# A two-block decoder on one core: mixer scores from plain fp32 data as head pairs, and the gated feed-forward's hidden part computed the other way round

## The chip, the cores and the metric

One core of a Trainium2 chip runs one program. The metric is the time of an execution on the device in microseconds (us). The kernel before was timed three times: median 1898.77 us (1898.02 to 1899.66). A separate execution was profiled.

## The reference, cut to what matters

256 tokens of width 1024 pass through 12 stages. Two layers of the first block, each: gated feed-forward, hybrid mixer, cross attention to a memory, gated feed-forward. Two layers of the second block, each: second mixer, feed-forward with squared ReLU. Before each stage stands an RMS norm, behind it another one and the residual sum. All data is fp32. The parts that the change touches:

```python
def swiglu(x, w_gate, w_up, w_down):            # w_gate, w_up: 1024 x 2816
    return (jax.nn.silu(x @ w_gate) * (x @ w_up)) @ w_down
# hybrid mixer: 8 query heads of 64, 2 key/value heads; keys and values also compressed
def compress(kv, pe, w1, w2):                   # 15 blocks of 32 tokens, per head
    ...
    return jax.nn.silu(flat @ w1) @ w2          # flat: 2048 wide, w1: 2048 x 256
s_c = einsum('bqgrd,bngd->bgrqn', qi, kc) * scale    # against 15 compressed keys
s_s = einsum('bqgrd,bqgmd->bgrqm', qi, ks) * scale   # against chosen blocks (here all)
s_w = einsum('bqgrd,bkgd->bgrqk', qi, kw) * scale    # against a window (here all)
# second mixer: 8 index heads and 8 attention heads of 64
logits = einsum('bqhd,bsd->bqhs', iq, ik) * 64 ** -0.5
s = einsum('bqhd,bqkhd->bqhk', q, k) * 64 ** -0.5
```

## The kernel before, in words

**Numbers.** TensorE has two ways of multiplying here. Weights and activations are split into two fp32r parts, high and low (`split`, L517; ScalarE writes the high part, VectorE the low one), and three products (high x low, low x high, high x high; `mm3`, L543) stand for one fp32 product. Plain fp32 operands are multiplied without a split; the profile shows each such product as two matmul records with a weight load each. A transpose is one record.

**Order.** The functions only record operations. `Recorder` (L145) then plans each engine's order with costs of its own (`cost`, L176) and buffers by tag (L499): 4 raw weight tiles, 6 each of `wH` and `wL`, and of the 8 PSUM banks 4 `acc`, 2 `mm`, 2 `tr`. Of the operations that are ready, TensorE takes the one recorded first. All loads go through SyncE's queue in program order. Every instruction is emitted at one line, L449, so groups are told apart by tiles.

**Weights.** `wunit` (L524) loads 256 rows of a weight matrix (512 KB) and splits them. `proj_gen` (L817) is a projection to up to 512 columns for both halves of 128 tokens: 4 units, and per half 24 matmuls with 512 columns, the activations `xT` as stationary operand. It yields after each unit, 8 times in all.

**Gated feed-forward** (`ffn`, L762; `ffn_like`, L708; four of the twelve stages). The 2816 hidden columns go in 11 chunks of 256. Chunk 0 uses `up` (L772): per token half 24 matmuls of 512 columns (gate and up side by side), SiLU and product on ScalarE and VectorE, and `hidden_T` (L755), two PE transposes and a split. Chunks 1 to 10 use `gemm_T` (L697): the weights are stationary and all 256 tokens move, so the hidden part comes out transposed, in 96 matmuls of 256 columns; `up_T` (L780) does the gating, for which `rstd_rows` (L688) makes a row copy of the norm factor, with two PE transposes per feed-forward. Then `down` of the chunk before takes 24 matmuls of 512 columns.

**Hybrid mixer** (`mix`, L993, two stages). Projections first, with `compress` (L1047) of keys and of values between them: 4 loads of 512 KB each, split; per load 8 matmuls of 256 columns whose stationary operand holds the high and the low part of the gathered blocks in 64 columns. Queries go to `stack` (L893): per parity of the heads one tile with the high part in one half of the 128 rows and the low part in the other. Keys (`dup_copy`, L1010) stand twice, high and low, in both halves of the rows. So a head's scores are two fp32r matmuls over 128 rows. Then per half of the tokens (L1203): compressed scores of 8 heads (8 records over `kcT`), softmax, and the head loop (L1240): scores against window and selected keys side by side (2 x 128 or 2 x 256 columns), softmax on VectorE and ScalarE, transposes, product with the values. `Fill` (L840) puts steps of other projections between the heads. Of the 4 `acc` banks, two hold the output sums, so two are left for scores.

**Second mixer** (`mix2`, L1327, two stages). Index scores (L1360): per head two fp32r matmuls, as above, with stacked queries. Attention (L1435): plain fp32 products over the 64 rows of a head; a group is two heads of the same parity, thus of the same half of the rows, in one bank. There are 4 groups per half of the tokens, with 128 keys for the first and 256 for the second.

## Time and profile before

| what | value |
|---|---|
| median of 3 runs | 1898.77 us |
| profiled execution, time | 1897.3 us |
| profiled execution, span | 1895.5 us |
| TensorE busy | 1873.8 us (99%) |
| TensorE clock granted | 0.999 of full speed |
| VectorE, ScalarE busy | 1260.9 us (67%), 1054.9 us (56%) |
| DMA | 332.13 MB, 54.4% of 16 engines' span |

The span is what the trace covers, from the first to the last instruction; the execution took 1.8 us more. A matmul's record is longer than the step to the next one, since matmuls are pipelined: what a matmul costs the stream is read from start to start.

### The profile page before, as it was taken

The page shows a single profiled execution, that of the slowest core. Times are in us where ns is not written, and L with a number is a line of the kernel's source. Part 1 is how long each engine was busy: PE and PEld are TensorE (multiplying, and loading weights), DVE is VectorE, ACT ScalarE, POOL GpSimd, SP SyncE. Part 2 cuts the span into 40 slices and gives each one's busy share as a digit, 9 for nine tenths or more (in the row PEclk, how much of TensorE's full clock was granted, in tenths as well). Part 3 has the DMA queues.
Part 4 walks back from the last instruction along what each step waited for, and adds up shares of the span by engine and source line. Part 5 has one row for each costly group of instructions (what it writes and reads, how often), then busy time and mean ns, then how long its engine had stood idle before and what let it go on. Part 6 is the DMA issues. An engine that isn't in the chain of part 4 may idle for free.

```text
span 1895.5 us, 30068 instructions
## 1 busy us (share of the span) xinstructions
PE 1873.8 (99%) x11452; PEld 1644.6 (87%) x11452; DVE 1260.9 (67%) x2194; ACT 1054.9 (56%) x1747; POOL 55.1 (3%) x82
## 2 busy tenths in 40 slices
PE   9999999999999999999999999999999999999998
PEld 7999788888999899988788889998789998788997
DVE  6655887766656665668967576557965556966554
ACT  5444775556444544457755664447665446565443
POOL 0000000200000000000011000000000000000000
PEclk9999999999999999999999999999999999999999
DMA  7555654454565566557444455565536555535653
GB/s 247 188 182 183 204 184 151 150 173 130 193 200 182 163 200 196 183 164 242 144 165 156 134 180 182 183 190 160 165 125 193 189 194 171 172 112 187 200 180 112
DMA packets 229569, 332.13 MB, mean 175 GB/s; under 512 B 17680, under 2 KB 123696, under 8 KB 229424
## 3 DMA queue, kind: packets, MB, share of 16 engines
q1 hardware_dynamic: 229424, 330.20, 54.4%
q8 instruction: 90, 1.47, 0.3%
q14 instruction: 55, 0.45, 0.1%
HBM read 329.10 MB, written 1.05 MB: 174 GB/s over the span
## 4 chain that ended last, share of the span: by engine, by line
PE 87%; DVE 7%; ACT 2%; DMA 2%; issue 1%; POOL 0%; SPq 0%; DVEq 0%; POOLq 0%; ACTq 0%
PE mm L449 36%; PE acc L449 31%; PE tr L449 20%; DVE wL L449 3%; DVE m L449 2%; ACT wH L449 1%; DVE s L449 1%; DVE sm L449 1%; DVE xT L449 1%; DMA raw<-in_w_in_dram 0%; DVE sc L449 0%; ACT xT L449 0%; DMA raw<-in_xa_wk_dram 0%; ACT junk L449 0%; DVE x L449 0%
## 5 line engine op out<-in xcount | busy, mean ns | idle before, releaser
L449 DVE TENSOR_TENSOR wL<-raw,wH 128x1024 fp32r<-128x1024 f32 (+3 forms) x612 | 732.1, 1200 | 235.0 <-ACT wH L449 231.6
L449 ACT ACTIVATE wH<-raw 128x1024 fp32r<-128x1024 f32 (+3 forms) x612 | 635.0, 1040 | 226.4 <-PE mm L449 92.6
L449 PE MATMUL acc<-wH,m 128*128 128x512 f32 (+1 forms) x1664 | 533.8, 392 | 0.6 <-DVE m L449 0.5
L449 PE MATMUL mm<-wH,xT 128*128 128x512 f32 (+2 forms) x1152 | 363.0, 384 | 6.2 <-DVE xT L449 3.5
L449 PEld LDWEIGHTS acc<-wH,m 128*128 128x128 f32 (+1 forms) x1664 | 309.0, 186 | 67.4 <-DVE m L449 2.4
L449 PE MATMUL acc<-wL,m 128*128 128x512 f32 (+1 forms) x864 | 331.6, 387 | 0.0
L449 PE MATMUL mm<-xT,wH 128*128 128x256 f32 x1792 | 323.0, 282 | 0.0
L449 PE MATMUL tr<-xT,wH 128*128 128x256 f32 x1664 | 299.1, 282 | 0.0
L449 PEld LDWEIGHTS mm<-xT,wH 128*128 128x128 f32 x1792 | 279.5, 190 | 3.7
L449 PEld LDWEIGHTS tr<-xT,wH 128*128 128x128 f32 x1664 | 259.1, 190 | 2.8
L449 PEld LDWEIGHTS mm<-wH,xT 128*128 128x128 f32 x1152 | 210.4, 188 | 49.5 <-DVE xT L449 10.0
L449 PE MATMUL mm<-xT,wL 128*128 128x256 f32 x896 | 250.6, 283 | 0.0
L449 PE MATMUL tr<-xT,wL 128*128 128x256 f32 x832 | 233.2, 283 | 0.0
L449 PE MATMUL mm<-wL,xT 128*128 128x512 f32 (+2 forms) x576 | 219.5, 381 | 0.4 <-DVE wL L449 0.2
L449 ACT ACTIVATE nat<-nat 128x512 f32<-128x512 f32 x68 | 42.9, 631 | 277.2 <-DVE nat L449 277.2
L449 PEld LDWEIGHTS acc<-wL,m 128*128 128x128 f32 (+1 forms) x864 | 159.0, 184 | 31.2
L449 PEld LDWEIGHTS mm<-xT,wL 128*128 128x128 f32 x896 | 169.3, 190 | 1.0
L449 PEld LDWEIGHTS tr<-xT,wL 128*128 128x128 f32 x832 | 157.4, 190 | 0.5
L449 PEld LDWEIGHTS mm<-wL,xT 128*128 128x128 f32 x576 | 108.5, 188 | 18.6 <-DVE wL L449 2.2
L449 POOL TENSOR_TENSOR sm<-sm,neghalf 128x1 f32<-128x1 f32 (+1 forms) x60 | 41.0, 683 | 1832.9 <-ACT sm L449 1678.4
L449 PE MATMUL mm<-wH,m 128*128 128x512 f32 x256 | 88.7, 406 | 0.0
L449 DVE TENSOR_TENSOR m<-acc,m 128x512 f32<-128x512 f32 (+1 forms) x64 | 39.7, 620 | 66.1 <-ACT junk L449 63.3
(158 smaller groups left out, 1610.7 us busy)
## 6 DMA issues: line engine op xcount, KB each, us to landing
raw<-in_w_ff_dram SPq DMA_DIRECT2D x128, 512.0 KB, 4.4
raw<-in_ffn_w_gate_dram SPq DMA_DIRECT2D x176, 256.0 KB, 3.4
raw<-in_ffn_w_up_dram SPq DMA_DIRECT2D x176, 256.0 KB, 3.8
raw<-in_ffn_w_down_dram SPq DMA_DIRECT2D x88, 512.0 KB, 5.3
raw<-in_w_in_dram SPq DMA_DIRECT2D x80, 512.0 KB, 4.0
raw<-in_w_out_dram SPq DMA_DIRECT2D x32, 512.0 KB, 3.6
raw<-in_cmp_w_dram SPq DMA_DIRECT2D x16, 512.0 KB, 4.6
raw<-in_xa_wk_dram SPq DMA_DIRECT2D x16, 512.0 KB, 5.7
```

Source lines behind the costliest of these rows:

```text
L449: getattr(getattr(self.nc, op.eng), op.name)(*[r(v) for v in op.args], **{k: r(v) for k, v in op.kw.items()})
```

## The change

The gated feed-forward no longer has an `up_T`: all its chunks use `up`, with weights moving in 512 columns and PE transposes of the hidden part. In the mixers queries and keys stay plain fp32 in 64 rows per head; two heads, one in each half of the rows, write to two banks one after the other (`SS`), and the second mixer's attention takes the two parities together likewise. `compress` multiplies plain data: each of four blocks of 128 rows has a stationary operand of 32 columns and writes its own 32 PSUM partitions; the four quarters are summed on VectorE. `compress` has become a generator that advances once per two steps of the query projection (keys) and of the gates' projection (values). The planner's cost of such matmuls is changed too. The diff, without some unchanged lines and four columns of indentation:

```diff
@@ -180,9 +180,11 @@
+        part = 0.6 if list(args[1].shadow.ap)[0][1] == 64 else 0.33 if m == 32 and n == 256 else 1.0
         if args[1].base.dtype == F32R or args[1].shadow.dtype == F32R:
             return max(0.4425 * n + 5.0, m / 1.2 + 4.0)
-        return 2 * max(2 * n / 2.4 + 3.0, m / 1.2 + 4.0)
+        return part * 2 * max(2 * n / 2.4 + 3.0, m / 1.2 + 4.0)
@@ -727,14 +730,14 @@
         h = T(tag, [128, nk, 256], F32R), T(tag, [128, nk, 256], F32R)
-        if c:
+        if c and up_T:
             banks = [P("mm" if c % 2 else "tr") for _ in range(2)]
...
             up_T([o.rearrange("p (j n) -> p j n", j=2) for o in banks], h, R)
-        for t in range(2 if c == 0 else 0):
-            if begin:
+        for t in range(0 if c and up_T else 2):
+            if c == 0 and begin:
@@ -777,15 +780,7 @@
-    def up_T(o, h, R):
-        g, hn = T("nat", [128, 2, 256]), T("nat", [128, 2, 256])
-        DVE.tensor_tensor(g, o[0], R, op=ALU.mult)
-        ACT.activation(g, g, AF.Silu)
-        DVE.tensor_tensor(g, g, R, op=ALU.mult)
-        DVE.tensor_tensor(hn, o[1], g, op=ALU.mult)
-        split(h[0], h[1], hn)
-    ffn_like(nch, load_up, up, up_T, load_down, 2, gains, xT, xTn, begin)
+    ffn_like(nch, load_up, up, None, load_down, 2, gains, xT, xTn, begin)
@@ -889,14 +884,6 @@
-def stack(dst, tr, t):
-    v, sl = tr.rearrange("p (k n) -> p k n", k=4), slice(t * 128, t * 128 + 128)
-    for par in range(2):
-        r, q = slice(par * 64, par * 64 + 64), slice(64 - par * 64, 128 - par * 64)
-        evict(dst[par][r, :, sl], v[r])
-        DVE.tensor_tensor(dst[par][q, :, sl], v[r], dst[par][r, :, sl].bitcast(F32), op=ALU.subtract)
@@ -994,7 +981,7 @@
-    KH, KL = (T("m4", [128, 2, 2, 256], F32R) for _ in range(2))
+    KK = T("m4", [128, 2, 2, 256])
@@ -1011,9 +998,8 @@
             r, q = slice(g * 64, g * 64 + 64), slice(64 - g * 64, 128 - g * 64)
-            for to in (r, q):
-                evict(KH[to, g, br, sl], tr[r, :])
-                DVE.tensor_tensor(KL[to, g, br, sl], tr[r, :], KH[r, g, br, sl].bitcast(F32), op=ALU.subtract)
+            evict(KK[r, g, br, sl], tr[r, :])
+            DVE.tensor_copy(KK[q, g, br, sl], tr[r, :])
@@ -1040,32 +1026,35 @@
                                   peT[:, q * 8:q * 8 + 8].unsqueeze(2).to_broadcast([128, 8, 15]), op=ALU.add)
-        GG = T("m4", [128, 16, 64], F32R)
-        split(GG[:, :, 0:32], GG[:, :, 32:64], G.rearrange("p j g n -> p j (g n)"))
-        return GG
-    def compress(i, GG):
+        return G
+    def compress(i, G, made):
         hp = P("acc")
...
             SP.dma_start(raw, a["cmp_w1"][l, i, u * 512:(u + 1) * 512, :].rearrange("(j p) n -> p j n", p=128))
-            H, L = T("wH", [128, 4, 256], F32R), T("wL", [128, 4, 256], F32R)
-            rec.background = True
-            split(H, L, raw)
-            rec.background = False
             for j in range(4):
-                k = 4 * u + j
-                PE.matmul(hp[:64, :256], GG[:, k, :], H[:, j, :], start=k == 0, stop=False)
-                PE.matmul(hp[:64, :256], GG[:, k, :], L[:, j, :], start=False, stop=k == 15)
+                PE.matmul(hp[32 * j:32 * j + 32, :256], G[:, 4 * u + j].rearrange("p g n -> p (g n)"), raw[:, j, :],
+                          start=u == 0, stop=u == 3, skip_group_check=True)
+            yield
         hn = T("hidn", [32, 256], bufs=2)
-        evict(hn, hp[32:64, :256])
-        DVE.tensor_tensor(hn, hn, hp[:32, :256], op=ALU.add)
+        evict(hn, hp[0:32, :256])
+        for r in (32, 64, 96):
+            DVE.tensor_tensor(hn, hn, hp[r:r + 32, :256], op=ALU.add)
         ACT.activation(hn, hn, AF.Silu)
...
         SP.dma_start(w2[:, :, 1, :], w2v)
-        return hn, w2
+        made += [hn, w2]
+    def side_by_side(proj_, other):
+        for i, _ in enumerate(proj_):
+            if i % 2:
+                next(other, None)
+        run(other)
@@ -1081,11 +1070,10 @@
     proj(w, 2840, 512, xT, dst_g)
-    hk, w2k = compress(0, GK)
-    qT = [T("m4", [128, 4, 256], F32R) for _ in range(2)]
+    qT = T("m4", [128, 4, 256])
@@ -1095,19 +1083,17 @@
                           rs.unsqueeze(2).to_broadcast([128, 8, 64]), op=ALU.mult)
-        tr = P("tr")
-        for k in range(4):
-            PE.transpose(tr[:, k * 128:k * 128 + 128], qn[:, k * 128:k * 128 + 128], ident)
-        stack(qT, tr, t)
-    proj(w, 0, 512, xT, dst_q)
+        transpose_f32(qT[:, :, t * 128:t * 128 + 128], qn, 4, on_act=True)
+    ck, cv = [], []
+    side_by_side(proj_gen(w, 0, 512, xT, dst_q), compress(0, GK, ck))
+    hk, w2k = ck
     hid = hidden(hk)
-    hv, w2u = compress(1, GV)
     kp = P("tr")
...
                   start=hf == 0, stop=hf == 1)
-    kc = T("kcT", [128, 2, 2, 16], F32R, bufs=1)
-    split(kc[:, :, 0], kc[:, :, 1], kp[:, :32].rearrange("p (g n) -> p g n", g=2))
+    kc = T("kcT", [128, 2, 16], bufs=1)
+    DVE.tensor_copy(kc, kp[:, :32].rearrange("p (g n) -> p g n", g=2))
@@ -1122,7 +1108,8 @@
     mT = memkv[("m", l)] = mem_prepare(l)
-    proj(w, 1024, 280, xT, dst_b2)
+    side_by_side(proj_gen(w, 1024, 280, xT, dst_b2), compress(1, GV, cv))
+    hv, w2u = cv
@@ -1205,17 +1192,18 @@
-        sc = P("acc")
-        for h in range(8):
-            PE.matmul(sc[:, h * 32:h * 32 + 32], qT[h % 2][:, h // 2, sl],
-                      kc[:, h // 4].rearrange("p r n -> p (r n)"), start=True, stop=True)
-        sv = sc[:, :256].rearrange("p (h r n) -> p h r n", h=8, r=2)
+        sc = [P("acc") for _ in range(2)]
+        for k in range(4):
+            for e in range(2):
+                r = slice(e * 64, e * 64 + 64)
+                PE.matmul(sc[e][:, k * 16:k * 16 + 16], qT[r, k, sl], kc[r, k // 2], start=True, stop=True)
         pc = T("s1", [128, 8, 32])
...
         pv = pc[:, :, 0:15]
-        DVE.tensor_tensor(pv, sv[:, :, 0, 0:15],
-                          cb[:, t * 16:t * 16 + 15].unsqueeze(1).to_broadcast([128, 8, 15]), op=ALU.add)
-        DVE.tensor_tensor(pv, pv, sv[:, :, 1, 0:15], op=ALU.add)
+        for e in range(2):
+            sv = sc[e][:, :64].rearrange("p (k n) -> p k n", k=4)
+            DVE.tensor_tensor(pc.rearrange("p (k e) n -> p k e n", e=2)[:, :, e, 0:15], sv[:, :, 0:15],
+                              cb[:, t * 16:t * 16 + 15].unsqueeze(1).to_broadcast([128, 4, 15]), op=ALU.add)
@@ -1239,10 +1227,14 @@
             g = h // 4
-            S = P("acc")
-            for i, KK in enumerate((KH, KL)):
-                PE.matmul(S[:, :2 * K].rearrange("p (b k) -> p b k", b=2), qT[h % 2][:, h // 2, sl],
-                          KK[:, g, :, 0:K], start=i == 0, stop=i == 1)
+            if h % 2 == 0:
+                SS = [P("acc") for _ in range(2)]
+                for e in range(2):
+                    r = slice(e * 64, e * 64 + 64)
+                    PE.matmul(SS[e][:, :2 * K].rearrange("p (b k) -> p b k", b=2), qT[r, h // 2, sl],
+                              KK[r, g, :, 0:K], start=True, stop=True)
+            S = SS[h % 2]
@@ -1327,8 +1319,8 @@
     idx = [T("m4", [128, 584]) for _ in range(2)]
-    iqT = [T("m4", [128, 4, 256], F32R) for _ in range(2)]
-    ikH, ikL = (T("ik", [128, 256], F32R, bufs=2) for _ in range(2))
+    iqT = T("m4", [128, 4, 256])
+    ik = T("ik", [128, 256])
@@ -1337,16 +1329,12 @@
             do_rope(idx[t][:, :576].rearrange("p (h d) -> p h d", d=64), t, 9)
-            tr = P("tr")
-            for k in range(4):
-                PE.transpose(tr[:, k * 128:k * 128 + 128], idx[t][:, k * 128:k * 128 + 128], ident)
-            stack(iqT, tr, t)
+            transpose_f32(iqT[:, :, t * 128:t * 128 + 128], idx[t][:, :512], 4, on_act=True)
             tr = P("tr")
...
             sl = slice(t * 128, t * 128 + 128)
-            for r in (slice(0, 64), slice(64, 128)):
-                evict(ikH[r, sl], tr[0:64, :128])
-                DVE.tensor_tensor(ikL[r, sl], tr[0:64, :128], ikH[0:64, sl].bitcast(F32), op=ALU.subtract)
+            evict(ik[0:64, sl], tr[0:64, :128])
+            DVE.tensor_copy(ik[64:128, sl], tr[0:64, :128])
@@ -1358,12 +1346,14 @@
         for h0 in (0, 1, 4, 5):
-            S = P("acc")
-            for j in range(2):
-                h = h0 + 2 * j
-                for i, kk in enumerate((ikH, ikL)):
-                    PE.matmul(S[:, j * K:j * K + K], iqT[h % 2][:, h // 2, sl], kk[:, 0:K],
-                              start=i == 0, stop=i == 1)
+            if h0 % 2 == 0:
+                SS = [P("acc") for _ in range(2)]
+                for j in range(2):
+                    for e in range(2):
+                        r = slice(e * 64, e * 64 + 64)
+                        PE.matmul(SS[e][:, j * K:j * K + K], iqT[r, h0 // 2 + j, sl], ik[r, 0:K],
+                                  start=True, stop=True)
+            S = SS[h0 % 2]
@@ -1433,12 +1423,15 @@
         for h0 in (0, 1, 4, 5):
-            S = P("acc")
+            if h0 % 2 == 0:
+                SS = [P("acc") for _ in range(2)]
+                for j in range(2):
+                    for e in range(2):
+                        r, hp = slice(e * 64, e * 64 + 64), h0 // 2 + j
+                        PE.matmul(SS[e][:, j * K:j * K + K], qT[r, hp, sl], kT[r, hp, 0:K], start=True, stop=True)
+            S = SS[h0 % 2]
             s = T("sc", [128, 2, K])
-            for j in range(2):
-                h = h0 + 2 * j
-                r = slice((h % 2) * 64, (h % 2) * 64 + 64)
-                PE.matmul(S[:, j * K:j * K + K], qT[r, h // 2, sl], kT[r, h // 2, 0:K], start=True, stop=True)
```

## Rows read from the trace of the kernel before

**Rows 1.** The page, parts 1 and 4: TensorE's busy row; the ending chain by engine.

```profile
PE 1873.8 (99%) x11452; PEld 1644.6 (87%) x11452; DVE 1260.9 (67%) x2194; ACT 1054.9 (56%) x1747; POOL 55.1 (3%) x82
...
PE 87%; DVE 7%; ACT 2%; DMA 2%; issue 1%; POOL 0%; SPq 0%; DVEq 0%; POOLq 0%; ACTq 0%
```

**Rows 2.** Ending chain in order of time: start us, length us, what; one chunk, ffn1.

```profile
58.31 11.42 PE mm L449 x96
69.73 5.58 PE acc L449 x24
```

**Rows 3.** PE timeline, an untransposed chunk: start us, us, instruction, count.

```profile
663.05 0.39 PE L449 MATMUL tr<-ident,s 128*128 128x128 f32 x2
663.19 0.48 PE L449 MATMUL mm<-wL,xT 128*128 128x512 f32 x1
663.51 0.63 PE L449 MATMUL mm<-wH,xT 128*128 128x512 f32 x2
```

**Rows 4.** PE timeline, second mixer's attention, scores with 128 keys, 64 rows.

```profile
1353.87 0.39 PE L449 MATMUL mm<-wH,xT 128*128 128x512 f32 x1
1354.19 0.71 PE L449 MATMUL acc<-m,m 64*128 64x128 f32 x4
1354.83 0.50 PE L449 MATMUL mm<-wH,xT 128*128 128x512 f32 x1
1355.16 0.39 PE L449 MATMUL mm<-wL,xT 128*128 128x512 f32 x1
```

**Rows 5.** PE timeline, the same with 256 keys.

```profile
1370.45 1.13 PE L449 MATMUL acc<-m,m 64*128 64x256 f32 x4
1371.51 0.50 PE L449 MATMUL mm<-wH,xT 128*128 128x512 f32 x1
```

**Rows 6.** PE timeline, first mixer, plain fp32 products with all 128 rows.

```profile
315.12 1.00 PE L449 MATMUL acc<-m,pT 128*128 128x64 f32 x8
315.93 0.48 PE L449 MATMUL mm<-wH,xT 128*128 128x512 f32 x1
316.24 0.39 PE L449 MATMUL mm<-wL,xT 128*128 128x512 f32 x1
```

**Rows 7.** PE timeline, first mixer, compression of the keys (32 records in all).

```profile
227.96 0.28 PE L449 MATMUL acc<-wH,m 128*64 128x256 f32 x1
...
231.65 0.40 PE L449 MATMUL mm<-wH,xT 128*128 128x512 f32 x1
```

**Rows 8.** PE timeline, first mixer, scores of the second tokens against compressed keys.

```profile
282.91 0.96 PE L449 MATMUL acc<-kcT,m 128*128 128x32 f32 x8
283.72 0.48 PE L449 MATMUL mm<-wH,m 128*128 128x512 f32 x1
284.04 0.39 PE L449 MATMUL mm<-wL,m 128*128 128x512 f32 x1
```

**Rows 9.** PE timeline, first mixer, one head's scores, 2 x 128 keys.

```profile
280.41 0.40 PE L449 MATMUL acc<-m,m 128*128 128x256 f32 x2
280.65 0.39 PE L449 MATMUL mm<-wH,m 128*128 128x512 f32 x1
```

**Rows 10.** PE timeline, first mixer, one head's scores, 2 x 256 keys.

```profile
308.17 0.71 PE L449 MATMUL acc<-m,m 128*128 128x512 f32 x2
308.72 0.40 PE L449 MATMUL mm<-wH,xT 128*128 128x512 f32 x1
```

**Rows 11.** PE timeline, second mixer, index scores with 256 keys.

```profile
1321.90 2.13 PE L449 MATMUL acc<-ik,m 128*128 128x256 f32 x14
1323.87 0.62 PE L449 MATMUL mm<-wH,xT 128*128 128x512 f32 x2
```

**Rows 12.** Who waited for whom, PE, whole span: us in total, times, longest us.

```profile
PE tr L449 <- DVE nat L449: 2.9, 5, 0.9
...
PE tr L449 <- DVE m L449: 1.3, 3, 0.5
```

**Rows 13.** DVE groups by form: count, busy us, mean ns, idle before: the weight splits.

```profile
L449 DVE TENSOR_TENSOR wL<-raw,wH 128x1024 fp32r<-128x1024 f32 x580 | 709.3, 1226 | 233.7 <-ACT wH L449 230.5
```

## What the change was predicted to do

> **What bounds the kernel.** I read the page first. TensorE is busy for 99% of the span, and the chain that ended last runs on it for 87% [rows 1]; the rest of that chain is short pieces at the seams. Then the chain in order of time: in the gated feed-forward it alternates 96 matmuls in 11.42 us and 24 in 5.58 us with nothing between [rows 2]. So the stream of TensorE is the time, and an edit is priced by what it adds to that stream or takes from it, start to start. Then the timeline, for the forms that the change adds. Two things are to be seen. First, leaving full-row matmuls for matmuls over 64 rows costs something. The fp32r matmul ahead of such a group takes 0.32 us to the next start, and the one behind it 0.33 [rows 4], where 0.23 is usual (5.58 / 24 [rows 2]); the group's four records take 0.64 [rows 4], where four full-row ones would take 4 x 0.111 = 0.45: eight of these take 0.81, and the next matmul 0.31, 0.08 too long [rows 6]. So 0.19 outside and 0.19 inside, 0.38 us per group of half-row matmuls. Full-row fp32 pays none of it [rows 6]. Second, a record costs 0.112 us at 128 columns and (1.06 - 0.19) / 4 = 0.216 at 256 [rows 5], so an estimate is 0.43 at 512; a plain product is two records.
>
> **The change, part by part.** The sum is made on the profiled execution, 1897.3 us, which is 1.5 under the median of the runs, 1898.77.
>
> *Gated feed-forward.* Chunks 1 to 10 of four stages: 96 matmuls, 11.42 us, go [rows 2]. In their place come 48 of 512 columns, twice the 24 of 5.58 us: 11.16 [rows 2]. To these come two pairs of transposes; a pair takes 0.14 us and makes the next matmul 0.32 instead of 0.23 long, 0.23 in all [rows 3]. That is 11.16 + 0.46 - 11.42 = +0.20 per chunk, +8.0 for 40 chunks. The two transposes of the row copy go in each stage, 4 x 0.23 = -0.9. Sum +7.1. VectorE and ScalarE lose work here, which TensorE's unbroken alternation already hid: worth nothing. Their new chain (SiLU, product, transposes, split) lies beside the other half's 24 matmuls or the `down` of the chunk before; without that cover it would show once per chunk.
>
> *Compression, per mixer.* Before, 32 matmuls in 3.69 us [rows 7], twice: 7.4. After, 8 groups of four products, two records of 0.216 each. Does the array run the four column quarters at once? No row shows it. Bounds: all at once 0.43 per group, one after the other 1.73. For entering the narrow form: nothing (the narrowest rows, 64 columns, enter and leave freely [rows 7], though over the whole array) or 0.38 as for half rows. I take all at once, since the four share neither operand nor partitions, and the 0.38, since these are tiles as the half rows are: 8 x 0.81 = 6.5, so -0.9. Ends: -4.0 and +9.5. With a free change of form the sum would be 16 x 0.38 = 6.1 us lower over both mixers. The Trainium skill (TensorEngine Tiling (Array Packing), Tiling Modes, Key Properties) says that changing the tiling mode drains the engine, and it names no exception for columns; that speaks against this change and for the sum with 0.38. Half rows agree with it [rows 4]; no row here shows narrow tiles.
>
> *Scores on half rows, per mixer.* Two heads of a pair use different halves and different banks; bounds are half of the serial time and all of it, and I take half, the rows' switch of 0.38 on top, since nothing is shared that a row shows to be busy. Compressed scores: before 0.81 + 0.08 per half of the tokens [rows 8], 1.8; after 2 x (8 x 0.112 + 0.38) = 2.6: +0.8 (serial +2.6). Head scores: before 0.24 per head [rows 9] and 0.55 [rows 10] less the 0.08 that a matmul behind transposes takes [rows 3], eight heads each: 1.9 + 3.7 = 5.6. After, four pairs per half: 4 x (0.43 + 0.38) + 4 x (0.86 + 0.38) = 8.2, +2.6 (serial 13.4, +7.8). So a first mixer changes by -0.9 + 0.8 + 2.6 = +2.5, two of them by +5.0.
>
> *Second mixer.* Index scores: before 16 x 0.14 [rows 11] and 16 x 0.11 [rows 8], 4.0; after two groups of four products per half, 2 x (0.45 + 0.38) + 2 x (0.86 + 0.38) = 4.1: +0.1 (serial +2.8). Attention: before four groups per half, each one switch: 4 x (0.45 + 0.38) + 4 x (0.86 + 0.38) = 8.3; after half as many groups with twice the products: 4.1, so -4.2 (serial 6.8, -1.5). Two mixers: -8.2.
>
> *What else moves.* The splits of 16 loads (1.23 us each on VectorE [rows 13], as much on ScalarE), half of the key copies, the query stacks and the split of the gathered blocks go: all beside TensorE's stream. The most that it can free are TensorE's waits for VectorE ahead of transposes, 2.9 + 1.3 us in the whole run [rows 12]; I book 0, as the copies that end them remain. The loads of `compress` now stand on SyncE's queue between the projection's, and a raw tile comes free only when TensorE has read it; each has a full step of the projection ahead of it. For the values they also stand behind the loads of the memory, which ran ahead of the gates' projection alone. On ScalarE the values' SiLU now comes among the gates' exponentials, and three small adds follow each compression; the steps of the other projections cover that. POOL's queue is passed by nothing.
>
> Sum: 7.1 + 5.0 - 8.2 = +3.9 us, 1901.2 in the profiled execution, **1902.7** as a median. A measurement of this kernel tells about 0.2%, 3.8 us, from no change, so this lies on the edge.
>
> **Rivals.** *Only neighbours overlap.* The two records of a product sit in the same tile, so if records start and end in their order, only the last of one head and the first of the next run together: n products take n + 1 record times, not n. Then compression takes 8 x (5 x 0.216 + 0.38) = 11.7 (+4.3), compressed scores +1.0, head scores 4 x (0.65 + 0.38) + 4 x (1.30 + 0.38) = 10.8 (+5.2), index scores +0.8, attention -3.5: 7.1 + 2 x 10.5 - 2 x 2.7 = +22.7, 1921. For it: all records of a form in the trace do follow one another. Against it: none of them had another half to run in. The Trainium skill (TensorE: Matmul & The Clock Gate, Part 3) says that matmuls start and end strictly in order while tiles overlap; by that rule it is this case, and no row here can show it.
>
> *Banks come free apart.* With two banks for scores, the second of a pair is free only when VectorE has read the odd head. Where TensorE has nothing recorded earlier to do, it takes the even head's product alone: each head is its own group. Head scores then take 8 x 0.81 + 8 x 1.24 = 16.4 (+10.8), and the attention gains nothing: 2 x (10.8 - 2.6 + 4.2) = +24.8 on the forecast, 1927. Against it: the projection steps between two pairs are recorded earlier and keep TensorE busy until both are free, as long as they don't run ahead. It decides from the point where softmax takes longer than these steps.
>
> *Not slower: columns switch for nothing and the seams close.* One mechanism: compression in quarters is free of drain and of splits. Then -6.1 for the switches and up to -4.2 for the waits of transposes [rows 12]: 3.9 - 10.3 = -6.4, 1892.4. For it: narrow operands pay nothing in rows 7. Against it: rows 4.
>
> **How the numbers follow.** Forecast 0.42, of which half within 0.2% and half above (own range 1896 to 1909); neighbours only 0.20; banks apart 0.12; columns free 0.20; pairs that don't overlap at all, with everything serial (7.1 + 2 x 19.9 + 2 x 1.3 = +49.5, 1948), 0.06. Faster by over 0.2% is the columns' case, 0.20; within is 0.22, half of the forecast's own and a hundredth of the others; slower is the rest, 0.58. The range, 1890 to 1922, holds the forecast, the neighbours' and the columns' case and leaves out the other two.
>
> **What would show it.** In the feed-forward a chunk of 17.00 us should become 17.20. A half-row pair with 256 columns each should take 0.43 + 0.19 us inside (0.65 + 0.19 with neighbours only), and a group of quarters 0.43 to 0.62 (1.08 and more). Attention of the second mixer should show two groups per half. Wrong would be: TensorE waiting for raw tiles in `compress`, heads of a pair that start far apart, or a chunk that is no longer than before.

## The result and the profile after

The changed kernel takes **1910.51 us** (median of six runs, 1905.09 to 1913.67) where the kernel before, run beside it, takes 1898.55: ratio **1.0061** [1.0048, 1.0075], 12.0 us slower. The forecast of 1902.7 was low by 7.8; the range, 1890 to 1922, holds the result, the forecast's own part of it, 1896 to 1909, does not, and slower by over 0.2% was the likeliest case. The six runs of the changed kernel lie in two groups that go with the mean granted clock: 1905.1 to 1907.7 us at 0.997 to 0.998, 1913.3 to 1913.7 at 0.993 to 0.994; the profiled execution (1913.67 us, span 1911.9) is of the second.

The page of the changed kernel, parts 1, 2 and 4, against [rows 1]:

```profile
PE 1893.2 (99%) x9716; PEld 1552.1 (81%) x9716; DVE 1186.0 (62%) x2146; ACT 1040.8 (54%) x1777; POOL 56.4 (3%) x82
...
PEclk9999979999999999999999999999999999999999
...
PE 92%; DVE 3%; DMA 2%; ACT 2%; issue 1%; SPq 0%; POOL 0%; DVEq 0%; POOLq 0%; ACTq 0%
```

TensorE has 1736 matmuls fewer and is busy 19 us longer; VectorE is relieved of 75 us, and the kernel is slower all the same. One digit of the granted clock (`PEclk`, in tenths, for 40 equal slices of the span), the sixth, is below 9.

The ending chain in order of time (start us, length us, what), one chunk of the first feed-forward, against [rows 2]:

```profile
58.21 7.13 PE mm L451 x31
65.34 0.22 PE tr L451 x2
65.56 3.91 PE mm L451 x17
69.47 1.86 PE acc L451 x8
71.33 0.22 PE tr L451 x2
71.55 3.72 PE acc L451 x16
```

The next chunk starts at 75.27: 17.06 us per chunk, where [rows 2] add up to 17.00 and 17.20 was forecast.

TensorE's timeline (start us, us, instruction, count; a row that starts in the window asked for is shown with the records up to the window's end). The first five rows are a group of column quarters and the matmuls around it; the `x4` is the same group seen through a window that ends 0.02 us after its start. Behind it stands the last group of the values in the same mixer, which came in three pieces. Then a single head of the first mixer's first half of the tokens, half of its compressed scores, a single head and a pair of the second half, and the second mixer's index scores and attention:

```profile
229.23 0.40 PE L451 MATMUL mm<-wH,xT 128*128 128x512 f32 x1
229.56 0.42 PE L451 MATMUL acc<-raw,m 128*32 128x256 f32 x4
229.56 0.64 PE L451 MATMUL acc<-raw,m 128*32 128x256 f32 x8
230.12 0.50 PE L451 MATMUL mm<-wH,xT 128*128 128x512 f32 x1
230.46 0.39 PE L451 MATMUL mm<-wL,xT 128*128 128x512 f32 x1
...
251.18 0.62 PE L451 MATMUL acc<-raw,m 128*32 128x256 f32 x2
...
252.32 0.63 PE L451 MATMUL acc<-raw,m 128*32 128x256 f32 x4
...
253.47 0.62 PE L451 MATMUL acc<-raw,m 128*32 128x256 f32 x2
...
285.56 0.70 PE L451 MATMUL acc<-m,m 64*128 64x256 f32 x2
286.19 0.50 PE L451 MATMUL mm<-wL,m 128*128 128x512 f32 x1
...
295.54 1.06 PE L451 MATMUL acc<-kcT,m 64*128 64x16 f32 x8
296.54 0.50 PE L451 MATMUL mm<-wH,m 128*128 128x512 f32 x1
...
311.44 1.12 PE L451 MATMUL acc<-m,m 64*128 64x512 f32 x2
312.50 0.44 PE L451 MATMUL tr<-ident,sc 128*128 128x128 f32 x2
...
323.77 1.13 PE L451 MATMUL acc<-m,m 64*128 64x512 f32 x4
324.83 0.44 PE L451 MATMUL tr<-ident,nat 128*128 128x128 f32 x2
...
1336.45 1.16 PE L451 MATMUL acc<-ik,m 64*128 64x128 f32 x8
1337.53 0.50 PE L451 MATMUL mm<-wL,xT 128*128 128x512 f32 x1
...
1376.80 0.71 PE L451 MATMUL acc<-m,m 64*128 64x128 f32 x8
1377.45 0.50 PE L451 MATMUL mm<-wH,xT 128*128 128x512 f32 x1
```

Three things are to be seen. The eight records of four quarters take 0.56 us to the next start, where two records of 0.216 one behind the other would be 0.43, and the matmuls around them take 0.33 and 0.34 instead of 0.23: the quarters overlap wholly, and of the switch of 0.38 they pay 0.13 inside and 0.21 outside. A pair of heads (four records of 512 columns, 1.06) takes no more than one head alone (two records, 1.06), so pairing halves the cost, where it happens. And in the first mixer it mostly doesn't happen: per mixer, all eight heads of the first half of the tokens stand alone (the row at 285.56 is one of them), two of eight do in the second half, and in one half two compressed groups of eight stand where one of sixteen was meant. The quarters are not safe from it either: of the eight groups of a mixer the last comes in three pieces with transposes between them, and each piece takes 0.55 to 0.56 us to the next start, as long as a whole group, so it costs some 1.1 us more per mixer.

TensorE's stretch around the dip of the clock: window us, length, busy us (and instructions) of PE, PEld, DVE, ACT, POOL, granted clock, DMA share, GB/s:

```profile
256.00:262.00 6.00, 4.72 (x23) 3.30 (x22) 4.76 (x11) 2.48 (x10) 1.86 (x4) 1.00 0.94 342
262.00:268.00 6.00, 4.68 (x10) 2.49 (x10) 4.41 (x11) 5.92 (x10) 0.00 (x0) 0.57 0.23 65
268.00:275.00 7.00, 7.00 (x17) 4.01 (x16) 2.68 (x17) 3.33 (x8) 0.00 (x0) 0.50 0.17 65
275.00:282.00 7.00, 7.00 (x20) 5.09 (x19) 4.01 (x15) 1.83 (x5) 0.00 (x0) 0.50 0.26 75
282.00:290.00 8.00, 8.00 (x42) 6.04 (x40) 5.48 (x24) 6.24 (x20) 0.00 (x0) 0.92 0.23 66
```

TensorE sits idle for 2.6 of the first 12 us, at the end of a stretch in which the DMA engines are nearly full (shares of 1.00, 0.87 and 0.94 in the three windows from 244 to 262 us; 0.78, 0.95 and 0.78 in the kernel before), and the clock falls and stays at its lower level, 1.2 GHz, for some 20 us. The rows lose 6 x 0.43 + 7 x 0.5 + 7 x 0.5 + 8 x 0.08 = 10.2 us of full speed. In the kernel before, the same place keeps its clock:

```profile
256.00:262.00 6.00, 5.18 (x30) 4.20 (x30) 5.42 (x11) 4.80 (x12) 1.87 (x4) 1.00 0.78 263
262.00:268.00 6.00, 5.53 (x29) 3.97 (x29) 5.54 (x25) 4.90 (x16) 0.05 (x1) 1.00 0.39 132
```

Stages, profiled against profiled, from the last transposes of `x` in one stage to those in the next (us, change against the kernel before; a stage that an edit leaves alone differs by up to 1.6 us between profiles): four feed-forwards +1.2, first mixers **+16.3** and +5.3, second mixers -3.6 and -3.4, all others under 0.4 each.

### The profile page after: what moved, and what is told of

Its sections match the earlier page's. It is cut to its first block, busy times and chain, and to the rows that moved or that the text cites. A ratio compares the mean times of both kernels' runs of the same rounds, so it can differ in the third digit from the quotient of the medians.

```text
span 1911.9 us, 26538 instructions
## 1 busy us (share of the span) xinstructions
PE 1893.2 (99%) x9716; PEld 1552.1 (81%) x9716; DVE 1186.0 (62%) x2146; ACT 1040.8 (54%) x1777; POOL 56.4 (3%) x82
## 3 DMA queue, kind: packets, MB, share of 16 engines
q8 instruction: 76, 1.25, 0.3%
HBM read 329.10 MB, written 1.05 MB: 173 GB/s over the span
## 4 chain that ended last, share of the span: by engine, by line
PE 92%; DVE 3%; DMA 2%; ACT 2%; issue 1%; SPq 0%; POOL 0%; DVEq 0%; POOLq 0%; ACTq 0%
PE mm L451 50%; PE acc L451 33%; PE tr L451 9%; DMA raw<-in_xa_wk_dram 1%; DVE wL L451 1%; ACT wH L451 1%; DVE m L451 1%; DMA raw<-in_ffn_w_up_dram 1%; DMA raw<-in_w_in_dram 0%; DVE xT L451 0%; ACT xT L451 0%; DVE s L451 0%; ACT junkx L451 0%; DVE sm L451 0%; SPq L451 0%
## 5 line engine op out<-in xcount | busy, mean ns | idle before, releaser
L451 DVE TENSOR_TENSOR wL<-raw,wH 128x1024 fp32r<-128x1024 f32 (+2 forms) x596 | 713.1, 1200 | 311.0 <-ACT wH L451 300.3
L451 ACT ACTIVATE wH<-raw 128x1024 fp32r<-128x1024 f32 (+2 forms) x596 | 618.6, 1040 | 294.9 <-PE mm L451 112.3
L451 PE MATMUL mm<-wH,xT 128*128 128x512 f32 (+2 forms) x2432 | 769.4, 389 | 2.8 <-ACT wH L451 1.2
L451 PEld LDWEIGHTS mm<-wH,xT 128*128 128x128 f32 x2432 | 451.1, 188 | 103.2 <-issue 6.4
L451 PE MATMUL acc<-wH,m 128*128 128x512 f32 x1600 | 522.5, 399 | 0.1
L451 PE MATMUL mm<-wL,xT 128*128 128x512 f32 (+2 forms) x1216 | 474.5, 390 | 1.0 <-DVE wL L451 0.9
L451 PEld LDWEIGHTS acc<-wH,m 128*128 128x128 f32 x1600 | 297.6, 188 | 64.6 <-DVE m L451 1.5
L451 PE MATMUL acc<-wL,m 128*128 128x512 f32 x800 | 315.9, 395 | 0.0
L451 PE MATMUL mm<-xT,wH 128*128 128x256 f32 x512 | 92.4, 282 | 0.0
L451 PEld LDWEIGHTS mm<-xT,wH 128*128 128x128 f32 x512 | 79.4, 190 | 1.7
```

Of the source, the lines that this page charges most:

```text
L451: getattr(getattr(self.nc, op.eng), op.name)(*[r(v) for v in op.args], **{k: r(v) for k, v in op.kw.items()})
```

## The experiments

Every kernel below computes the whole reference. Ratios are against the kernel before, run on the same chip. The planner's new cost stands in all of them but the first, and was not tried by itself.

**Each part alone.** Four kernels are the kernel before with one part of the change.

> The kernel before with the gated feed-forward's edit alone. Theory A (the forecast's term: 48 matmuls of 512 columns at 0.2325 us and two pairs of transposes in place of 96 at 0.119): +7.1 us, chunks of 17.20 us. Theory B (read from the changed kernel's trace, where a chunk is 17.06 us): +1 to +2 us.

```diff
-        if c:
+        if c and up_T:
...
-    ffn_like(nch, load_up, up, up_T, load_down, 2, gains, xT, xTn, begin)
+    ffn_like(nch, load_up, up, None, load_down, 2, gains, xT, xTn, begin)
```

Measured: 1895.52 us, 0.9984 [0.9974, 0.9993], -2.7 (-4.9 to -1.3). The sum's largest term, +7.1, is refuted. Its profile shows the four feed-forwards at +1.1 together, as theory B has it, but the time lies below theory B too. PE's waits, the kernel before first, then this one (us in total, times, longest):

```profile
PE mm L449 <- DVE xT L449: 3.5, 6, 0.9
```

```profile
PE mm L449 <- DVE xT L449: 0.8, 3, 0.4
```

Three waits of 0.9 us went, all of them behind a feed-forward, where the next stage's first matmuls wait for the normalized activations.

> The kernel before with the second mixer's edit alone. Theory A (groups of both halves of the rows overlap in full, half as many switches): -8.2 us over both stages. Theory B (as in the changed kernel's trace, where some groups hold one half only): -7 us. Theory C (neighbours only overlap): -5.4 us.

```diff
-        for h0 in (0, 1, 4, 5):
-            S = P("acc")
+            if h0 % 2 == 0:
+                SS = [P("acc") for _ in range(2)]
...
+                            PE.matmul(SS[e][:, j * K:j * K + K], qT[r, hp, sl], kT[r, hp, 0:K], start=True, stop=True)
```

Measured: 1889.23 us, 0.9954 [0.9939, 0.9969], -9.0 (-11.6 to -5.9); forecast -8.2. Theory C's -5.4 lies outside; the time doesn't tell A from B. The trace is B's: in both stages the index scores of the first half stand in groups of eight records.

> The kernel before with compression in quarters, stepped beside the projections, alone; scores as before. Theory A (matmuls only: 8 groups of 0.57 + 0.19 us against 7.4 us per mixer): -2.6 us, the clock unchanged. Theory B (raw tiles stay taken until TensorE has read them, so the loads of the memory's key weights come late): TensorE waits for these loads behind the gates' projection, 2 to 3 us per mixer, so +2 to +4 us, and where the wait lets the granted clock fall to its lower level in a stretch, some runs about 8 us more.

```diff
-                PE.matmul(hp[:64, :256], GG[:, k, :], H[:, j, :], start=k == 0, stop=False)
-                PE.matmul(hp[:64, :256], GG[:, k, :], L[:, j, :], start=False, stop=k == 15)
+                PE.matmul(hp[32 * j:32 * j + 32, :256], G[:, 4 * u + j].rearrange("p g n -> p (g n)"), raw[:, j, :],
+                          start=u == 0, stop=u == 3, skip_group_check=True)
```

Measured: 1898.82 us, 1.0002 [0.9993, 1.0012], +0.6 (-1.3 to +2.3), where -1.8 was forecast. Theory A's -2.6 lies outside, theory B's +2 just inside; the clock does not fall. Its groups are whole, all sixteen, and yet its first mixers are 1.7 and 1.1 us longer in the profile, with TensorE idle for 2.3 us more in them together (8.1 instead of 5.8). Waits of the stage thus eat what the groups save in part; the rest is within what such a stage differs anyway.

> The kernel before with the first mixer's scores as head pairs alone; compression as before. Theory A (pairs stay together, as the forecast had it): +3.4 us per mixer, +7 in all. Theory B (banks come free apart, so heads run alone as in the changed kernel's trace, 0.63 + 0.19 us per head with 2 x 128 keys against 0.24): +7 to +9 us per mixer by the count of groups, +14 to +18 in all, less what VectorE's and ScalarE's saved splits give back.

```diff
-    KH, KL = (T("m4", [128, 2, 2, 256], F32R) for _ in range(2))
+    KK = T("m4", [128, 2, 2, 256])
...
+                for e in range(2):
+                    r = slice(e * 64, e * 64 + 64)
+                    PE.matmul(SS[e][:, :2 * K].rearrange("p (b k) -> p b k", b=2), qT[r, h // 2, sl],
+                              KK[r, g, :, 0:K], start=True, stop=True)
```

Measured: 1915.96 us, 1.009 [1.007, 1.011], **+17.8**, where +6.8 was forecast: theory B. TensorE's timeline shows the first mixer's heads of the first half of the tokens: one pair and six single heads (one of each stands here), then a compressed group of eight. For the second half its heads stand in four pairs.

```profile
268.07 0.70 PE L451 MATMUL acc<-m,m 64*128 64x256 f32 x4
...
270.99 0.70 PE L451 MATMUL acc<-m,m 64*128 64x256 f32 x2
...
288.28 1.06 PE L451 MATMUL acc<-kcT,m 64*128 64x16 f32 x8
```

The four parts add up to -2.7 - 9.0 + 0.6 + 17.8 = +6.7 of the +12.0.

**Keeping pairs together.** `joint` records the products of a pair or a group as one operation, which needs all its banks at once.

> The changed kernel with each group of both halves recorded as one operation, so that TensorE takes it only when both banks are free and its products stand together. Theory A (heads that run alone are what the first mixer lost): 8 groups of 0.82 us fewer in the first half of the tokens over both mixers, 2 of 1.25 in the second half, and 4 groups of compressed and index scores of 1.2 each: 12 to 14 us less than the changed kernel. Theory B (TensorE now waits for the second bank, so what is saved comes back as waits): no change within 3 us.

```diff
-                for e in range(2):
-                    r = slice(e * 64, e * 64 + 64)
-                    PE.matmul(SS[e][...], qT[r, h // 2, sl], KK[r, g, :, 0:K], start=True, stop=True)
+                both = []
+                for e in range(2):
+                    r = slice(e * 64, e * 64 + 64)
+                    both.append(((SS[e][...], qT[r, h // 2, sl], KK[r, g, :, 0:K]), dict(start=True, stop=True)))
+                rec.joint(both)
```

Measured: 1895.57 us, 0.9989 [0.998, 0.9999]: with all parts of the change and the same matmuls, only taken together, the kernel stands at -1.8 us instead of +12.0: theory A. The first mixers stand at +4.5 and +3.2, the second at -6.3 and -4.2. The quarters were not joined: the values' last group still comes in three pieces in both mixers.

> The kernel before with the second mixer's edit alone and its groups kept together. Theory A (full overlap whenever the halves stand together): groups of the index scores with 128 keys and the odd groups of the attention join, 0.6 to 1 us per stage on top of the edit alone: -8 to -9 us against the kernel before. Theory B (waiting for both banks costs as much as it saves): as the edit alone, -7 us.

Measured: 1886.7 us, 0.9946 [0.9931, 0.9961], -10.7 (-13.1 to -7.4). Theory B's -7 lies outside, theory A's -8 to -9 inside. Against the edit alone, at -9.0, the two intervals overlap; that the groups joined is seen in the rows. In the changed kernel the index scores of the first half fell into groups of eight records at 1.08 us each, eight record times, so without any overlap; joint, sixteen take 1.09:

```profile
1315.65 1.16 PE L481 MATMUL acc<-ik,m 64*128 64x128 f32 x16
1316.74 0.51 PE L483 MATMUL mm<-wL,xT 128*128 128x512 f32 x1
```

> The first mixer's scores on row halves alone, as in the run that had them at +17.8 us, but with each pair's two products, and the 16 records of the compressed scores, kept together. Theory A (all that was above the forecast was pairs that came apart): the forecast's +0.8 and +2.6 per mixer, +6.8, 1905 us. Theory B (part of it is something else in the stage): by subtraction from the run of the whole change with joint groups (-1.8, less -2.7, +0.6 and -10.7) +11, 1909 to 1910 us. Theory C (pairing gains nothing): 1916 us.

Measured: 1904.84 us, 1.0033 [1.0022, 1.0044], **+7.5**: theory A. The kernel differs from the one at +17.8 by `joint` alone, so 10.3 us of the loss of this part are pairs that came apart. In the changed kernel more heads stand alone than in the one at +17.8. Its timeline has every pair and both compressed groups whole:

```profile
277.88 0.70 PE L481 MATMUL acc<-m,m 64*128 64x256 f32 x4
278.51 0.50 PE L483 MATMUL mm<-wH,m 128*128 128x512 f32 x1
...
288.98 1.07 PE L481 MATMUL acc<-kcT,m 64*128 64x16 f32 x16
289.97 0.66 PE L483 MATMUL acc<-m,pT 128*128 128x64 f32 x4
```

By groups: 12 single heads that become 6 pairs save 6 x (0.63 + 0.19) = 4.9 us in both mixers, two compressed groups fewer 2 x (1.00 + 0.19) = 2.4; where the other 3.0 of the 10.3 come from was not traced.

**The compression's place, and the clock.** Three kernels are the changed kernel with one edit each.

> The changed kernel with each compression in one piece at its old place (ahead of the query projection and of the memory's loads) in place of steps between a projection's. Theory A (stepping the values' compression beside the gates' projection crowds the loads of the memory's key weights): the wait of 2 to 3 us per mixer behind the gates' projection goes, the clock stays at its upper level: 5 us less than the runs of the changed kernel at 0.997, 12 less than those at 0.994. Theory B (the plain groups read raw tiles wherever they stand): the waits move to the place of compression and the time stays within 3 us.

```diff
-    side_by_side(proj_gen(w, 0, 512, xT, dst_q), compress(0, GK, ck))
+    run(compress(0, GK, ck))
+    proj(w, 0, 512, xT, dst_q)
+    run(compress(1, GV, cv))
...
-    side_by_side(proj_gen(w, 1024, 280, xT, dst_b2), compress(1, GV, cv))
+    proj(w, 1024, 280, xT, dst_b2)
```

Measured: 1909.88 us, 1.0067 [1.0052, 1.0082], no better than the changed kernel: theory B. The timeline (in brackets: idle before, and what ended it) shows where the wait has gone:

```profile
226.44 1.93 PE L451 MATMUL acc<-raw,m 128*32 128x256 f32 x32
232.07 1.22 PE L451 MATMUL mm<-wH,xT 128*128 128x512 f32 x2 [3.70 <-ACT wH L451]
```

All 32 records of the keys' compression run in under 2 us as one group, then TensorE waits 3.7 us for the projection's weights, which stand behind the compression's loads, and goes on at the lower clock.

> The changed kernel with five raw tiles in place of four. Theory A (raw tiles held by compression are what makes the memory's key weights late): the wait behind the gates' projection shrinks by at least 1 us per mixer and the clock does not fall: 2 to 4 us less, and 10 less than runs whose clock fell. Theory B (that stretch is bound by the DMA engines' share of 1.0): no change.

```diff
-    BUFS = dict(raw=4, wH=6, ...)
+    BUFS = dict(raw=5, wH=6, ...)
```

Measured: 1909.89 us, 1.0068 [1.0051, 1.0085]: nothing gained, theory B. The DMA engines are nearly full as before (a share of 0.97 in the window 256 to 262 us).

> The changed kernel, with the compression of the values beside the gates' projection of 512 columns ahead of the queries', instead of beside the 280-column projection behind the loads of the memory. Theory A (the stretch at half the clock in the first mixer follows TensorE's gap of 3.4 us at 259 to 263 us, and the gap comes from four more loads in a stretch in which the DMA engines are already full): gap about 1 us as in the kernel before, no granted clock of half speed behind it, mean granted clock 0.998 or more, the first mixer about 10 us shorter than in the changed kernel's profile, median 1903 to 1906 us. Theory B (the stretch has another cause, or the loads' queue moves the gap elsewhere): a gap of 2 us or more somewhere between 220 and 265 us, mean granted clock 0.994 to 0.997, median 1908 to 1913 us.

```diff
-    proj(w, 2840, 512, xT, dst_g)
+    side_by_side(proj_gen(w, 2840, 512, xT, dst_g), compress(1, GV, cv))
...
-    side_by_side(proj_gen(w, 1024, 280, xT, dst_b2), compress(1, GV, cv))
+    proj(w, 1024, 280, xT, dst_b2)
```

Measured: **1898.46 us**, 1.0006 [0.9997, 1.0015], +1.1 instead of +12.0 and better than theory A's 1903 to 1906. Here the values go beside the 512-column projection (the diff's first line), and the projection behind the memory's loads, of 280 columns, runs alone. Its windows:

```profile
250.00:256.00 6.00, 3.94 (x32) 3.32 (x31) 3.50 (x5) 4.61 (x9) 0.55 (x1) 0.78 0.54 187
256.00:262.00 6.00, 6.00 (x18) 4.73 (x19) 5.90 (x11) 5.94 (x13) 0.97 (x2) 0.65 0.88 302
262.00:268.00 6.00, 5.02 (x29) 3.33 (x27) 4.55 (x19) 3.55 (x10) 1.01 (x3) 1.00 0.52 152
```

Theory A was half right. (The gap of 3.4 us that it starts from is not one gap: eight transposes, 1.3 us together, stand in it.) TensorE's idle time was not taken away: it is 2.1 us of the first window, and the clock falls there too. But it is back by 262 us, with 6 x 0.22 + 6 x 0.35 = 3.4 us lost instead of 10.2. The first mixers stand at +7.3 and +3.6 where the changed kernel has +16.3 and +5.3, 10.7 us less. The clock is 6.8 of it in the profiles. The move has also changed TensorE's order: per mixer the heads stand in 7 and 4 groups for the two halves of the tokens, instead of 8 and 5, which by the groups is 2 x (0.82 + 1.25) = 4.1 us, and the values' last group is whole. So the place of the values' loads and matmuls costs the changed kernel some 11 us, but not through the clock alone; what keeps the clock low for some 20 us in one and some 7 in the other stays open. The earlier place together with joint pairs was not run.

**Do the good parts add up?**

> The kernel before with two parts of the change: the feed-forward with transposed products, and the second mixer's head pairs in row halves with each pair's group kept together; the first mixer stays as it was. Theory A (the parts are independent): -2.7 us of the feed-forward alone and -10.7 of the second mixer with joint groups make -13.4, 1885 us (1883 to 1888), granted clock 0.999. Theory B (the feed-forward's gain was seams that fell well in that one schedule): 1888 us, the second mixer's gain alone.

Measured: **1882.48 us**, 0.9916 [0.9903, 0.993], -14.9: theory A, a little beyond it. This version beats both kernels by more than their intervals: the feed-forward and the joint second mixer, with the first mixer untouched. TensorE is busy for 1860.4 us of its span of 1881.8.

> The feed-forward and the joint second mixer as in the run of this call that has those two, with the compression in column quarters added, keys beside the queries' projection, values beside the gates'. Theory A (a compression in quarters saves what the groups show, 7.4 less 8 x 0.81 us per mixer, once its loads don't stand in the full stretch): 1.8 us less than the run without it, 1883 us. Theory B (what a mixer gains in the stream goes to waits, as when it was done alone at +0.6 us): the same as or up to 2 us more than the run without it, 1885 to 1887 us.

Measured: 1891.76 us, 0.9969 [0.9958, 0.998], **9.3 us slower** than the run without the quarters; neither theory had that. First mixers: +5.6 and +3.2 against it, with 5.2 us more idle time of TensorE in the two together and 5.1 us lost to the clock. Windows of the first mixer, the run without the quarters first:

```profile
250.00:256.00 6.00, 6.00 (x50) 5.80 (x49) 4.52 (x6) 4.58 (x8) 0.42 (x1) 1.00 0.88 312
256.00:262.00 6.00, 5.22 (x28) 4.14 (x28) 5.86 (x12) 5.80 (x13) 1.85 (x4) 1.00 0.81 246
```

```profile
250.00:256.00 6.00, 4.31 (x33) 3.78 (x32) 4.07 (x8) 4.51 (x10) 0.55 (x1) 0.96 0.84 282
256.00:262.00 6.00, 5.44 (x17) 4.27 (x18) 5.90 (x11) 5.25 (x10) 0.00 (x0) 0.50 0.62 214
```

The waits are named in its timeline:

```profile
254.37 1.07 PE L483 MATMUL acc<-kcT,m 128*128 128x32 f32 x8 [0.67 <-DVE kcT L483]
255.90 1.94 PE L483 MATMUL tr<-ident,nat 128*128 128x128 f32 x8 [0.46 <-DVE nat L483]
258.40 0.80 PE L483 MATMUL mm<-wH,m 128*128 128x512 f32 x1 [0.56 <-DVE m L483]
```

Two costs are visible. The gaps: TensorE waits for the compressed keys and then for the memory's data, and is idle for 1.7 us of the first window, where the run without the quarters is busy throughout. And the clock, 6 x 0.04 + 6 x 0.50 = 3.2 us. Whether it is the earlier place of the values or the quarters themselves that opens these gaps was not tried apart on this kernel. On the kernel before, the quarters at the later place cost +0.6 us, and in the changed kernel the earlier place saved some 11, so the place alone does not decide.

## Why the prediction was right, and where its steps failed

The range and the side came out, but that is in good part luck, since errors of both signs met (the sum of the last column takes the first two terms as measured alone):

| term of the sum | forecast | measured alone | groups kept together |
|---|---|---|---|
| feed-forward | +7.1 | -2.7 | |
| compression | -1.8 | +0.6 | |
| first mixer's scores | +6.8 | +17.8 | +7.5 |
| second mixer | -8.2 | -9.0 | -10.7 |
| sum | +3.9 | +6.7 | -5.3 |
| all parts in one kernel | | +12.0 | -1.8 |

- **What bounds the kernel**: right. TensorE is busy for 99% and the chain runs on it for 92% instead of 87%.
- **Feed-forward, mis-sized.** A term of the sum failed, "48 of 512 columns, twice the 24 of 5.58 us: 11.16". In the chain these 48 take 7.13 + 3.91 = 11.04, 0.230 each instead of the 0.2325 of `down`, and two pairs of transposes 0.44. So a chunk is 17.06, +0.06 and not +0.20, and a difference of 0.0025 us per matmul, between two different places of the kernel, was multiplied by 1920: 40 x 0.06 - 0.9 = +1.5 instead of +7.1; the profile has +1.1. The second step that failed is that VectorE's and ScalarE's relief is "worth nothing": waits for `xT` at the seams fell from 3.5 to 0.8 us. With +1.1 that makes -1.6, inside the interval of that run, -4.9 to -1.3 us; what makes the rest down to -2.7, if it is more than spread, is not shown.
- **Compression, right in the groups, wrong in the stage.** All at once plus 0.38 was taken, 0.81 per group; measured is 0.56 to the next start and 0.2 outside. The first rival (only neighbours overlap) is refuted by the `x4` row, and the third (columns switch for nothing) by the matmuls around the group. The rule on draining at a change of tiling mode (Trainium skill, TensorEngine Tiling (Array Packing), Tiling Modes, Key Properties) holds for columns as for rows here: the four 32-column tiles pay 0.34 us per group. The sentence "each has a full step of the projection ahead of it" failed: with the edit alone TensorE is idle for 2.3 us more in the two stages, and the 1.8 us of the forecast are not saved. That the nearly full DMA engines make it wait is argued from their shares, 0.86 to 1.05 in that run from 244 to 262 us.
- **Scores on half rows: the price was right, the schedule wrong.** Kept together they cost +7.5 against +6.8 forecast. In the changed kernel the second rival, banks that come free apart, holds for the first half of the tokens and a quarter of the heads of the second, and not in the attention. In the run of this part alone it costs 10.3 us, of the 24.8 that the rival had for both mixers. That it is the banks that part the two heads is read from the planner's rule; the runs show only that keeping them together removes the cost. What was said against it, that earlier steps "keep TensorE busy until both are free", failed: TensorE took the even head's product alone. It had a chance of 0.12; the two banks and the rule "the one recorded first" in the kernel before were reason for more.
- **Second mixer**: attention has two groups per half, 0.65 us at 128 keys [rows 4], as the last part of the prediction said, but for one half of one stage, where a group fell into three. The index scores with 128 keys lost their overlap, 1.09 + 0.19 us per stage; the two halves of `ik` are copied by ScalarE and VectorE one after the other, which may be why, but that was not tried. Joint groups take the stages from -4.3 and -3.6 us to -6.3 and -4.7 in the profiles.
- **Terms that were missing: the clock, and what the parts do to each other's order.** +12.0 less +6.7 leaves 5.3 us that no part has alone, and the changed kernel's profile shows more than enough for it. The lower level of the clock costs 10.2 us in the first mixer of the profiled execution, where no part alone lost more than 1.7. And more stands apart than in the parts: per mixer one group of heads more in each half of the tokens than in the run of the scores alone, 4.1 us over both mixers, and the values' last group in three pieces instead of one, some 2.2. How the 5.3 divide between these is not shown. With the groups kept together 3.5 us are left likewise, -1.8 against -5.3, and that profile has 3.4 us of lower clock in the first mixers and the three pieces too. The prediction named "TensorE waiting for raw tiles in `compress`" as a sign of being wrong, but priced a gap at its own length only, and not at what follows it.

## What to carry to other kernels

A gain from tiles that run side by side exists only if their instructions are issued side by side: make a pair one unit for the scheduler, above all when its outputs come free at different times. An idle time of TensorE may cost more than its length, by what the granted clock does behind it, so read the clock's windows after moving loads: four loads at another place saved some 11 us in one kernel here and came with a loss of 9 in another. When one term is a small difference times a large count, take its durations from the same form at the same place, and test the parts alone: here the best kernel (0.9916) is the change without its first mixer, and with the groups of the second kept together.

## What was not expected of the hardware

- The four quarters' first records start within 0.02 us of each other, and the second records follow together: a plain fp32 product's two records do not stand between its neighbours'. The Trainium skill (TensorE: Matmul & The Clock Gate, Part 3) describes tiles that start a few ns apart; the trace agrees, with 6 to 7 ns from one quarter to the next. The prediction's rival had taken the two records of a product to stand next to each other, and that is what the trace refutes.
- Two heads in different row halves overlap wholly, which the forecast had taken without a row to show it: a pair's group takes 0.63 us at 256 columns and 1.06 at 512, as long as one head alone.
- How little idle time stands ahead of a fall of the clock. From 256 to 268 us TensorE was idle for 1.3 us in the kernel before and for 1.4 us in the one with the compression alone, and both kept 2.4 GHz; for 1.4 us in the kernel with joint pairs, which fell to 1.2 GHz for some 3 us; for 2.6 us in the changed kernel, which fell for some 20; at 228 to 232 us, after 3.7 us at a stretch, the kernel with each compression in one piece fell for some 7. The idle time tells neither whether the clock falls nor for how long, and no rule is drawn from these rows.
